# Down stages in slots, split halves made earlier, and another order of the first block-product step in a streaming encoder layer

## The chip, the core and the metric

The kernel runs on one core of one Trainium2 chip. Its time is the device time of one execution in microseconds (us), the median of several runs. TensorE (PE) multiplies, VectorE (DVE) and ScalarE (ACT) work elementwise and read the accumulators in PSUM, GpSimd (POOL) works elementwise on SBUF alone, and the queue of SyncE (SP) issues the DMAs. The engines run side by side, each in its own program order, and wait for each other by semaphores.

## The reference

One step of an encoder layer for 1056 rows (1024 of a prompt, 32 of a running stream), width 1024. Two SwiGLU feed-forward blocks (FFN) of inner width 2816 enclose a token mixer:

```python
def swiglu(h, w_gate, w_up, w_down):
    return (jax.nn.silu(h @ w_gate) * (h @ w_up)) @ w_down

def layer(x, lw, sb_fn, s0, gla_chunk):
    ...
    x = x + 0.5 * swiglu(rmsnorm(x, g_ffn1), w1g, w1u, w1d)
    mix, k, v, s = token_mixer(rmsnorm(x, g_mix), w_in, w_gate_up, ...)
    x = x + mix
    x = x + 0.5 * swiglu(rmsnorm(x, g_ffn2), w2g, w2u, w2d)
    return rmsnorm(x, g_final), k, v, s
```

The mixer (stick-breaking attention beside gated linear attention) is not touched by the change.

## The kernel before, in words

All data lie transposed: `x[d]` and `h[d]` (d of 8) hold 128 features by 1056 rows. A float32 value is kept as two halves, a rounded high one and the rest: ScalarE copies the high half, VectorE subtracts to get the low half, and a product is made of three matmuls (high by high, high by low, low by high). Such a pair of instructions is called a split (`split_to`, L96, its ScalarE copy at L100, its VectorE subtraction at L104; in slots L50 and L51).

An FFN has these stages.

*Opening.* The first pair of hidden tiles (f = 0 and 1) is multiplied plainly, row quarter by row quarter (`Opening`, matmuls at L292). Beside it the normed `x` is split into `h` and `X` (tiles `h` and `part`), and the sums T1, T3, T2, T4 of its blocks are made and split (`Halves.part`, sums L243, splits L104).

*Gate and up.* The other 20 hidden tiles are made in 20 steps (a gate step and an up step for each pair i = 1 to 10), each a seven-product block scheme (`Step`, matmuls L384): product p multiplies a weight sum with a block sum (`PRODUCTS`) and adds into one of four PSUM banks a, b, c, d. Products 1 and 2 share bank a, 7 and 4 share c, 5 and 3 share d, and 6 has b. `ORDER` is 1, 6, 7, 5, 2, 4, 3. After each product VectorE or ScalarE reads a bank (`after`): c1 after 1, u2 = c1 + b after 6 (L400), u3 = u2 + c after 7 (L403), outputs after 5, 2, 4 and 3. The second product of a bank adds to what stands there, so it must wait until the first has been read out. Within these steps the program order is written out by hand (`manual_schedule`): `Slots` is a list of work by product number, where `later(k)` puts work k products on. `slots.split` puts the ScalarE half at k and the VectorE half at k + 1. The weights' sums of the next step are made on GpSimd in the same way. In the first FFN the slots also carry the splitting of the mixer's weights (`Splits`: load, split, store to `win_split` and `wo_split`). Pairs 1 to 8 are kept as block sums in DRAM (`keep`, `part_spill`); the six plain tiles 0, 1 and 18 to 21 (`PLAIN`) go to `hid_spill` unsplit.

*Down.* Pairs 1 to 8, in four groups of two, are multiplied by the down weights in 16 steps (`DownStep`, matmuls L590, banks `pd_a` to `pd_d`), again of seven products, here of 12 matmuls. VectorE reads each bank (L579) and GpSimd adds (L608). Between the products stand the loads of later weights (`wraw`) and parts, the sums on GpSimd (L553 to L556) and the splits of the next step (`prep`). In the last group `plain_tile` and `plain_slab` load and split the six plain tiles (12 halves) and six slabs of their weights. This stage has no hand-written order: a scheduler places the instructions of each engine.

*Plain.* The six plain tiles are multiplied by their slabs (`pd`, L109 to L111). The second FFN ends with the closing norm.

Of the kernel before, what the change touches and what calls it, by code (L numbers as in the profile page):

```python
# [533 lines left out]
PLAIN = (0, 1, 18, 19, 20, 21)  # L534


class DownStep:
# [6 lines left out]
    def sums(self, raw):  # L544
# [6 lines left out]
        s1, s2, s3, s4 = s12[:, :w], s12[:, w:], s34[:, :w], s34[:, w:]  # L551
        self.src = raw, s12, s34
# [5 lines left out]
    def halves(self):  # L558
        S = self.S
        w = 2 * P  # L560
        raw, s12, s34 = self.src
        tag = ("S1", "A22") if self.odd else ("S2", "S3")
        wa = S.sr.tile([P, 2, 512], F32R, name=tag[0], tag=tag[0])
        wb = S.sr.tile([P, 2, 512], F32R, name=tag[1], tag=tag[1])
        ws = S.wp.tile([P, 2, 1024], F32R, name="whl", tag="w")
# [5 lines left out]
        self.W = {"A11": cut(wa, 0), "A12": cut(wa, 1), "A22": cut(wb, 0)}  # L571
        self.W.update({f"S{i + 1}": cut(ws, i) for i in range(4)})
# [39 lines left out]
class Down:  # L612
# [25 lines left out]
    def load_w(self, pool, name):  # L638
        t = pool.tile([P, 1024], F32, name=name, tag=name)
        self.S.nc.sync.dma_start(t, self.src[self.slab])  # L640
        self.slab += 1
        return t
# [1259 lines left out]
```

## Time and profile before

| what | value |
|---|---|
| time, median of 3 runs | 2134.49 us (2132.89 to 2135.83) |
| the profiled execution | 2135.43 us, span 2133.5 us |
| TensorE busy | 2058.4 us, 96% of the span |
| VectorE, ScalarE, GpSimd busy | 67%, 42%, 31% |
| mean granted clock of TensorE | 0.99 |
| first FFN: first `L384` matmul, first `L590`, first plain `pd` | 76.39, 496.86, 671.48 us |
| second FFN: the same | 1468.25, 1877.96, 2050.41 us |

The trace is of one execution. A row of the timeline has start, length, engine, line, operation, output and inputs, shapes and count; in brackets stands how long the engine was idle before it and what ended that. Matmul lengths overlap, so a product's time is the distance between starts.

### The profile page before, as it was taken

To read this page: it belongs to the slowest core of one execution; us is meant where nothing else is said; L and a number is where in the kernel's file an instruction comes from. 1 tells how busy PE (TensorE), PEld (TensorE's weight loads), DVE (VectorE), ACT (ScalarE), POOL (GpSimd) and SP (SyncE) were. 2 spreads that over 40 slices of the span, in tenths; PEclk is the share of its full clock that TensorE was granted. 3 is DMA by queue.
4 is the path that set the end of the run, shared out by engine and by line. 5 is a ranking of instruction groups with operands and counts; after the bars stand their busy time and mean duration, and the time that the engine had idled before them with its cause. 6 is when DMAs were issued, how large, how long until landed. Compare 5 with 4: busy or idle time off the path is not lost.

```text
span 2133.5 us, 38802 instructions
## 1 busy us (share of the span) xinstructions
PE 2058.4 (96%) x15636; PEld 1991.8 (93%) x15636; DVE 1438.7 (67%) x2205; ACT 886.8 (42%) x1618; POOL 655.3 (31%) x578
## 2 busy tenths in 40 slices
PE   7899999999999999999999999899999999999997
PEld 6899999999999988888989988899999999999997
DVE  6767777765786656286766688596666666467855
ACT  6544444442233443235555565353333433322333
POOL 0034433435773200111121201101343343357720
PEclk9999999999999999999999999999999999999999
DMA  5156776779653211113314152331243434597322
GB/s 175 55 212 249 254 259 250 248 257 386 246 194 115 76 67 60 44 64 86 91 49 134 54 182 75 106 109 49 108 155 138 152 132 151 188 376 290 113 65 82
DMA packets 128339, 325.03 MB, mean 152 GB/s; under 512 B 12097, under 2 KB 32865, under 8 KB 124833
## 3 DMA queue, kind: packets, MB, share of 16 engines
q1 hardware_dynamic: 128160, 322.56, 42.8%
q8 instruction: 123, 2.02, 0.4%
q14 instruction: 56, 0.45, 0.1%
HBM read 201.72 MB, written 114.03 MB: 148 GB/s over the span
## 4 chain that ended last, share of the span: by engine, by line
PE 80%; DVE 9%; issue 3%; DMA 3%; ACT 3%; POOL 2%; DVEq 0%; SPq 0%; ACTq 0%; POOLq 0%
PE acc_a L384 11%; PE acc_c L384 11%; PE acc_d L384 11%; PE acc_b L384 6%; PE acc L292 4%; PE pj L109 4%; PE pj L111 3%; PE pj L110 3%; PE pd_a L590 2%; PE pd_d L590 2%; PE pd_c L590 2%; PE pd L109 2%; PE pd L111 2%; PE pd L110 2%; DMA wraw<-hid_spill 2%
## 5 line engine op out<-in xcount | busy, mean ns | idle before, releaser
L384 PE MATMUL acc_a<-h,whl 128*128 128x264 f32 x1920 | 249.9, 286 | 8.4 <-DVE whl L104 8.4
L384 PEld LDWEIGHTS acc_a<-h,whl 128*128 128x128 f32 x1920 | 241.5, 190 | 8.6 <-DVE whl L104 8.6
L384 PE MATMUL acc_d<-part,S 128*128 128x264 f32 x1920 | 246.1, 284 | 0.0
L384 PEld LDWEIGHTS acc_d<-part,S 128*128 128x128 f32 x1920 | 238.4, 188 | 0.0
L109 PE MATMUL pj<-h,whl 128*128 128x352 f32 x576 | 204.7, 355 | 0.0
L111 PE MATMUL pj<-h,whl 128*128 128x352 f32 x576 | 189.9, 330 | 0.0
L110 PE MATMUL pj<-h,whl 128*128 128x352 f32 x576 | 188.3, 327 | 0.0
L434 POOL TENSOR_TENSOR x<-tc,x 128x528 f32<-128x528 f32 x60 | 100.7, 1678 | 181.4 <-DVE tc L433 139.9
L50 ACT ACTIVATE x<-x 128x528 fp32r<-128x528 f32 (+1 forms) x164 | 102.5, 635 | 113.8 <-issue 30.2
L51 DVE TENSOR_TENSOR x<-x 128x528 fp32r<-128x528 f32 (+1 forms) x164 | 129.9, 805 | 17.4 <-ACT x L50 17.4
L355 POOL TENSOR_TENSOR s<-wraw 128x512 f32<-128x512 f32 x38 | 58.1, 1529 | 225.9 <-DVE S L104 186.4
L384 PE MATMUL acc_c<-h,A 128*128 128x264 f32 x960 | 124.2, 285 | 0.0
L384 PE MATMUL acc_b<-h,S 128*128 128x264 f32 x960 | 124.2, 285 | 0.0
L384 PE MATMUL acc_c<-part,S 128*128 128x264 f32 x960 | 123.0, 284 | 0.0
L384 PEld LDWEIGHTS acc_c<-h,A 128*128 128x128 f32 x960 | 120.4, 188 | 0.0
L384 PEld LDWEIGHTS acc_b<-h,S 128*128 128x128 f32 x960 | 120.4, 188 | 0.0
L384 PEld LDWEIGHTS acc_c<-part,S 128*128 128x128 f32 x960 | 119.2, 188 | 0.0
L608 POOL TENSOR_TENSOR x<-x,u 128x528 f32<-128x528 f32 x64 | 98.7, 1549 | 53.0 <-DVE x L579 52.0
L109 PEld LDWEIGHTS pj<-h,whl 128*128 128x128 f32 x576 | 109.8, 191 | 4.8 <-issue 1.5
L50 ACT ACTIVATE S<-s 128x512 fp32r<-128x512 f32 x152 | 93.4, 623 | 46.9 <-PE acc_b L384 18.4
L51 DVE TENSOR_TENSOR S<-s,S 128x512 fp32r<-128x512 f32 x152 | 112.1, 738 | 0.0
L111 PEld LDWEIGHTS pj<-h,whl 128*128 128x128 f32 x576 | 109.2, 190 | 1.9 <-issue 1.0
(349 smaller groups left out, 4886.2 us busy)
## 6 DMA issues: line engine op xcount, KB each, us to landing
part_spill<-x SPq DMA_DIRECT2D x112, 528.0 KB, 3.4
h<-part_spill SPq DMA_DIRECT2D x64, 528.0 KB, 10.4
part<-part_spill SPq DMA_DIRECT2D x48, 528.0 KB, 10.6
win_split<-x SPq DMA_DIRECT2D x44, 512.0 KB, 3.4
whl<-win_split SPq DMA_DIRECT2D x22, 1024.0 KB, 4.9
wraw<-w1g SPq DMA_DIRECT2D x22, 512.0 KB, 5.3
wraw<-w1u SPq DMA_DIRECT2D x22, 512.0 KB, 6.3
x<-win SPq DMA_DIRECT2D x44, 256.0 KB, 3.1
```

What stands on the lines that cost most here:

```text
L50: self.later(k, lambda: nc.scalar.activation(hi, src, AF.Copy))
L51: self.later(k + 1, lambda: nc.vector.tensor_sub(lo, src, hi.bitcast(F32)))
L109: nc.tensor.matmul(out, w[:, 0, wsl], a[:, 0, asl], start=first, stop=False)
L110: nc.tensor.matmul(out, w[:, 0, wsl], a[:, 1, asl], start=False, stop=False)
L111: nc.tensor.matmul(out, w[:, 1, wsl], a[:, 0, asl], start=False, stop=last)
L292: nc.tensor.matmul(out, self.w[i](k, a), quarter(S, k, b, j), start=k == 0 and n == 0, stop=k == KT - 1 and n == 2)
L355: eng.tensor_add(self.s1, a21, a22)
L384: nc.tensor.matmul(t[:, s, :SW], w[:, a, ks], m(k, b, s), start=fresh and k == 0 and n == 0, stop=k == 3 and n == 2, skip_group_check=not ...
L434: nc.gpsimd.tensor_mul(two(hid), t, sg)
L590: nc.tensor.matmul(t[:, s, :SW], w[:, u, k * P : k * P + P], b[:, v, ss(s)], start=fresh and k == 0 and i == 0, stop=k == 1 and i == 2, sk ...
L608: nc.gpsimd.tensor_add(x[r][h], x[r][h], u)
```

## The change

- `FIRST`: the first gate step of each FFN makes its products in the order 1, 5, 2, 6, 7, 4, 3. The output of product 5's quarter is then read out after product 7.
- The sums T2 and T4, and the weights' sums of the first step, are emitted later or in another order. In the first FFN T2 comes behind the weights of product 5, T4 behind the Opening in both.
- In the down stages everything on TensorE, VectorE, ScalarE and SP, loads included, has a written order. The sums and splits of the next step come in two parts (`first`, `second`) by slots, between the products of the step before.
- Tiles 18 and 19 are split in gate and up, when they are made, and stored as halves (`hid_split`). In the second FFN tiles 0 and 1 and the six slabs are also split there, by `Splits`, as jobs of 512 or 528 columns (`halves_of`), and stored (`hid_split`, `w2d_split`); the down stage then loads the halves. The other splits of the last group stay, in slots.

The diff, cut:

```diff
+def halves_of(jobs):
+
+    out = []
+    for src, dst in jobs:
+        w = src.shape[-1] // 2
+        out += [(src[:, h * w : h * w + w], dst[:, :, h * w : h * w + w]) for h in range(2)]
+    return out
...
-        for n in range(2 * len(self.jobs)):
+        dma = self.S.nc.sync.dma_start
+        for n, (src, out) in enumerate(self.jobs):
             k = 5 * n // 2
-            buf = self.bufs[n % 2][:, :1024]
+            w = src.shape[-1]
+            buf = self.bufs[n % 2][:, : 2 * w]
             t = buf.rearrange("p (a n) -> p a n", a=2)
             hl = t.bitcast(F32R)
-            src, out = self.jobs[n // 2]
-            cols = slice(n % 2 * 512, n % 2 * 512 + 512)
-            dma = self.S.nc.sync.dma_start
-            slots.later(k, lambda buf=buf, src=src, cols=cols: dma(buf[:, 512:], src[:, cols]))
-            slots.split(hl[:, 0], hl[:, 1], buf[:, 512:], k + 2, lambda t=t, out=out, cols=cols: dma(out[:, :, cols], t))
+            raw = buf[:, w:]
+            slots.later(k, lambda raw=raw, src=src: dma(raw, src))
+            slots.split(hl[:, 0], hl[:, 1], raw, k + 2, lambda t=t, out=out: dma(out, t))
...
 ORDER = (1, 6, 7, 5, 2, 4, 3)
+FIRST = (1, 5, 2, 6, 7, 4, 3)
...
+            if "d" in A:
+                self.out(3, self.u3, A["d"])
...
+            if "c" in A:
+                self.out(3, self.u3, A["d"])
...
-            if f in PLAIN:
+            if f in PLAIN and f not in SPLIT:
...
+        if 2 * self.i in SPLIT:
+            q = {"B11": 0, "T1": 1, "B21": 2, "B22": 3}.get(name)
+            if q is not None:
+                out = self.S.hid2[PLAIN.index(2 * self.i + q // 2)][:, :, q % 2 * HALF : q % 2 * HALF + HALF]
+                self.keep(out, self.S.x[4 + q][:, :HALF])
+            return
...
-                for p in (6, 7, 5):
-                    prep(p)
+                prep(5)
+                between(4, 0)
+                prep(6)
+                prep(7)
...
     for k in range(4):
         H.part("T3", k, 1)
+    for k in range(4):
+        H.part("T4", k)
...
-            for n, p in enumerate(ORDER):
+            for n, p in enumerate(ORDER if t else FIRST):
...
+SPLIT = (18, 19)
...
-        nc.gpsimd.tensor_add(s1, a[3], a[2])
-        nc.gpsimd.tensor_sub(s2, s1, a[0])
-        nc.gpsimd.tensor_sub(s3, a[0], a[3])
-        nc.gpsimd.tensor_sub(s4, a[1], s2)
...
-        split_to(S, wa[:, 0], wa[:, 1], raw[:, :512])
-        split_to(S, ws[:, 0, :512], ws[:, 1, :512], s12)
-        split_to(S, wb[:, 0, :w], wb[:, 1, :w], raw[:, 2 * w : 3 * w])
-        split_to(S, ws[:, 0, 512:], ws[:, 1, 512:], s34)
...
+        nc.gpsimd.tensor_add(s12[:, :w], a[3], a[2])
+        nc.gpsimd.tensor_sub(s12[:, w:], s12[:, :w], a[0])
...
+        S.slots.split(self.wa[:, 0], self.wa[:, 1], raw[:, :512], k)
+        S.slots.split(self.ws[:, 0, :512], self.ws[:, 1, :512], s12, k + 1)
...
+        nc.gpsimd.tensor_sub(s34[:, :w], a[0], a[3])
+        nc.gpsimd.tensor_sub(s34[:, w:], a[1], s12[:, w:])
+        S.slots.split(self.wb[:, 0, :w], self.wb[:, 1, :w], a[2], k)
+        S.slots.split(self.ws[:, 0, 512:], self.ws[:, 1, 512:], s34, k + 1)
...
-            self.steps[0].sums(self.raw.pop(0))
+            self.steps[0].first(self.raw.pop(0), 1)
         elif p == 5:
             self.load_part(0, 6)
-        elif p == 2:
-            self.steps[0].halves()
...
-        for i, st in enumerate(self.steps):
-
-            def between(n):
-                if n == 0:
-                    self.load_step(i + 2)
-                if n == 1:
-                    self.prep(i + 1)
-                if st.g < last and n % 2 == 0 and 4 * (n // 2) + st.m < 7:
-                    self.load_part(st.g + 1, 4 * (n // 2) + st.m)
-                if st.g == last and n % 2 == 0 and n < 6:
-                    self.plain_tile(3 * st.m + n // 2)
-                if st.g == last and n == 5 and st.m > 1:
-                    self.plain_slab()
-
-            st.emit(between)
+        todo = [(lambda n=n: self.plain_tile(n)) for n in range(12)]
+        at = {}
+        for n, fn in enumerate(todo):
+            at[12 + n // 4, n % 4 * 2] = fn
+        for j, key in enumerate(((13, 1), (15, 0), (15, 1), (15, 2), (15, 3))):
+            at[key] = lambda j=j: self.plain_slab(j)
+        E = mybir.EngineType
+        with S.tc.manual_schedule(engines={E.PE, E.DVE, E.Activation, E.Pool, E.SP}):
+            for i, st in enumerate(self.steps):
+
+                def between(n):
+                    S.slots.run()
+                    if n == 0:
+                        self.load_step(i + 2)
+                    if i + 1 < len(self.steps):
+                        if n == 0:
+                            self.steps[i + 1].first(self.raw.pop(i + 1), 1)
+                        if n == 1:
+                            self.steps[i + 1].second(2)
+                    if st.g < last and n % 2 == 0 and 4 * (n // 2) + st.m < 7:
+                        self.load_part(st.g + 1, 4 * (n // 2) + st.m)
+                    if (i, n) in at:
+                        at[i, n]()
+                    S.slots.now += 1
+
+                st.emit(between)
+            self.plain_slab(5)
+            while S.slots.at:
+                S.slots.run()
+                S.slots.now += 1
...
-        raw = S.raw2.tile([P, 1024], F32, name="wraw2", tag="wraw2")[:, :HALF]
-        S.nc.sync.dma_start(raw, S.hidden[n // 2][:, cols])
-        t = self.tiles[n // 2]
-        split_to(S, t[:, 0, cols], t[:, 1, cols], raw)
-
-    def plain_slab(self):
+        t = self.tiles[n // 2][:, :, cols]
+        if PLAIN[n // 2] in SPLIT or PLAIN[n // 2] < 2 and self.done is not None:
+            S.nc.sync.dma_start(t.bitcast(F32), S.hid2[n // 2][:, :, cols])
+        else:
+            S.nc.sync.dma_start(t[:, 1].bitcast(F32), S.hidden[n // 2][:, cols])
+            S.slots.split(t[:, 0], t[:, 1], t[:, 1].bitcast(F32), 3)
...
-        split_to(S, w[:, 0], w[:, 1], r)
+        if self.done is not None:
+            S.nc.sync.dma_start(w.bitcast(F32), self.done[j])
+        else:
+            pool, name = (S.raw, "wraw") if j in (0, 1, 3, 5) else (S.raw2, "wraw2")
+            raw = pool.tile([P, 1024], F32, name=name, tag=name)
+            S.nc.sync.dma_start(raw, self.src[len(self.steps) + j])
+            S.slots.split(w[:, 0], w[:, 1], raw, 3)
...
-                    emit(parts(H))
+                    emit(parts(H, "T1", "T3"))
+                if j == 4:
+                    emit(parts(H, "T2"))
...
+            splits = Splits(S, halves_of(jobs), (S.x[2], S.x[3]))
...
-            down = Down(S, A["w2d"])
+            down = Down(S, A["w2d"], A["w2d2"])
+            jobs = [(S.hidden[i], S.hid2[i]) for i in range(2)] + [(A["w2d"][16 + j], A["w2d2"][j]) for j in range(6)]
+            splits = Splits(S, halves_of(jobs), (S.x[2], S.x[3]))
...
+                    emit(parts(H, "T1", "T3", "T2"))
+
+            gate_up(S, H, op, steps, lambda j, n: [], between, down.head, xs, splits.plan)
```

How instructions move. First VectorE in the first FFN, at the end of the Opening (`x<-x` are the block sums, `h` T2's and T4's splits, `whl` the weights of products 1 and 2, `S` and `A` weight sums, `hid` an output of the Opening). Before:

```order
L243 TENSOR_TENSOR x<-x 128x528 x6
L104 TENSOR_TENSOR h_84<-x,h_84 128x528
L104 TENSOR_TENSOR h_85<-x,h_85 128x528
L104 TENSOR_TENSOR h_86<-x,h_86 128x528
L243 TENSOR_TENSOR x<-x 128x528 x3
L104 TENSOR_TENSOR h_87<-x,h_87 128x528
L104 TENSOR_TENSOR h_88<-x,h_88 128x528
L104 TENSOR_TENSOR h_89<-x,h_89 128x528
L243 TENSOR_TENSOR x<-x 128x528 x2
L304 TENSOR_TENSOR hid<-sg,acc_615 128x528
L104 TENSOR_TENSOR h_90<-x,h_90 128x528
L104 TENSOR_TENSOR h_91<-x,h_91 128x528
```

and now, from the same place on:

```order
L253 TENSOR_TENSOR x<-x 128x528 x3
L314 TENSOR_TENSOR hid<-sg,acc_615 128x528
L113 TENSOR_TENSOR whl<-wraw,whl 128x1024
L113 TENSOR_TENSOR S_766<-s_764,S_766 128x512
L253 TENSOR_TENSOR x<-x 128x528 x3
L113 TENSOR_TENSOR h_84<-x,h_84 128x528
L113 TENSOR_TENSOR h_85<-x,h_85 128x528
L113 TENSOR_TENSOR h_86<-x,h_86 128x528
L253 TENSOR_TENSOR x<-x 128x528
L113 TENSOR_TENSOR S_788<-s_786,S_788 128x512
L314 TENSOR_TENSOR hid<-sg,acc_791 128x528
L113 TENSOR_TENSOR h_87<-x,h_87 128x528
```

Before, `whl` is the row behind these; now it stands third, and T4's sums and splits come further on.

TensorE in the first step, with product 7 (`acc_c` from `part`) and what follows it. Before, product 5 in `acc_d`:

```order
L384 MATMUL acc_c<-part_104,S_797 128x264 x6
L384 MATMUL acc_c<-part_105,S_797 128x264 x6
L384 MATMUL acc_d<-part_106,S_800 128x264 x6
L384 MATMUL acc_d<-part_107,S_800 128x264 x6
L384 MATMUL acc_d<-part_106,S_800 128x264 x6
```

and now product 4, in the bank of product 7:

```order
L394 MATMUL acc_c<-part_104,S_788 128x264 x6
L394 MATMUL acc_c<-part_105,S_788 128x264 x6
L394 MATMUL acc_c<-h_88,A_864 128x264 x3
L394 MATMUL acc_c<-h_89,A_864 128x264 x3
L394 MATMUL acc_c<-h_90,A_864 128x264 x3
```

VectorE there, now (`u_987` is u2, `u_1019` u3, `A` and `h` what product 4 needs, the rows at L51 the first piece of `win` and a weight sum of the next step):

```order
L113 TENSOR_TENSOR A_864<-wraw_529,A_864 128x512
L378 TENSOR_TENSOR s_867<-wraw,s_781 128x512
L113 TENSOR_TENSOR h_91<-x,h_91 128x528
L410 TENSOR_TENSOR u_987<-s_903,acc_b 128x528
L113 TENSOR_TENSOR S_869<-s_867,S_869 128x512
L51 TENSOR_TENSOR x<-x 128x512
L51 TENSOR_TENSOR S_933<-s_931,S_933 128x512
L413 TENSOR_TENSOR u_1019<-u_987,acc_c 128x528
L437 TENSOR_TENSOR x<-u_1019,acc_d 128x528
L437 TENSOR_TENSOR x<-u_987,acc_c 128x528
```

From the start of the list of now above, 33 short instructions and `whl` stand ahead of u3, the read-out of `acc_c`; before, u3 stood behind the splits of T2 and T3 and had two products to itself.

VectorE in the last group of the down stage of the first FFN (`whl` with `s`, `S` and `A` are splits of the next step's weights, `part_106` a slab, `h_85` a plain tile, the rows with `pd` read-outs). Before:

```order
L104 TENSOR_TENSOR whl<-s_7150,whl 128x512
L104 TENSOR_TENSOR whl<-s_7151,whl 128x512
L104 TENSOR_TENSOR part_106<-wraw,part_106 128x1024
L579 SCALAR_TENSOR_TENSOR u_7148<-pd_b,s_7127 128x528
L579 SCALAR_TENSOR_TENSOR tc<-pd_c,u_7148 128x528
L579 SCALAR_TENSOR_TENSOR x<-pd_d,x 128x528
L579 SCALAR_TENSOR_TENSOR x<-pd_a,x 128x528
L104 TENSOR_TENSOR S_7288<-wraw_7129,S_7288 128x512
```

and now:

```order
L600 SCALAR_TENSOR_TENSOR u_7291<-pd_b,s_7265 128x528
L51 TENSOR_TENSOR h_85<-h_85 128x528
L600 SCALAR_TENSOR_TENSOR tc<-pd_c,u_7291 128x528
L51 TENSOR_TENSOR S_7274<-wraw_7139,S_7274 128x512
L600 SCALAR_TENSOR_TENSOR x<-pd_d,x 128x528
L51 TENSOR_TENSOR h_85<-h_85 128x528
L51 TENSOR_TENSOR whl<-s_7270,whl 128x512
L600 SCALAR_TENSOR_TENSOR x<-pd_a,x 128x528
L51 TENSOR_TENSOR S_7275<-wraw_7139,S_7275 128x256
L600 SCALAR_TENSOR_TENSOR x<-pd_c,x 128x528
L51 TENSOR_TENSOR whl<-s_7271,whl 128x512
L51 TENSOR_TENSOR part_106<-wraw,part_106 128x1024
```

Three splits in a row ahead of two read-outs have become one or two splits behind each read-out.

## Rows read from the trace of the kernel before

**Rows 1.** Busy time by stretches: PE, PEld, DVE, ACT, POOL, clock, DMA.

```profile
85.20:496.80 411.60, 411.58 (x3358) 411.59 (x3359) 290.54 (x379) 174.79 (x290) 162.70 (x112) 0.99 0.69 247
496.80:671.50 174.70, 167.48 (x1347) 165.91 (x1346) 133.02 (x172) 52.51 (x90) 116.96 (x108) 0.99 0.64 233
...
1878.00:2050.40 172.40, 165.87 (x1346) 164.17 (x1344) 132.28 (x171) 52.37 (x90) 116.96 (x104) 1.00 0.64 232
...
1468.20:1878.00 409.80, 409.80 (x3363) 409.80 (x3362) 238.64 (x323) 147.64 (x239) 155.30 (x111) 1.00 0.40 148
```

**Rows 2.** Waits of TensorE: us in total, times, longest.

```profile
PE pd_c L590 <- DVE tc L579: 9.2, 8, 1.9
```

**Rows 3.** Timeline of TensorE, first step of the first FFN.

```profile
76.39 0.41 PE L384 MATMUL acc_a<-h,whl 128*128 128x264 f32 x2
85.22 5.00 PE L384 MATMUL acc_a<-h,whl 128*128 128x264 f32 x22 [8.42 <-DVE whl L104]
...
107.61 0.65 PE L384 MATMUL acc_a<-h,whl 128*128 128x264 f32 x4
```

**Rows 4.** Timeline of VectorE and GpSimd, same place.

```profile
71.26 3.80 DVE L243 TENSOR_TENSOR x<-x 128x528 f32<-128x528 f32 x6
...
83.94 1.22 DVE L104 TENSOR_TENSOR whl<-wraw,whl 128x1024 fp32r<-128x1024 f32 x1
...
86.50 1.27 POOL L355 TENSOR_TENSOR s<-wraw 128x512 f32<-128x512 f32 x1 [85.66 <-DVE S L104]
86.90 3.30 DVE L104 TENSOR_TENSOR part<-x,part 128x528 fp32r<-128x528 f32 x4
```

**Rows 5.** The chain that ended last, same product of two steps.

```profile
98.98 2.93 PE acc_a L384 x24
...
119.47 2.93 PE acc_a L384 x24
```

**Rows 6.** Stretches about waits; granted clock is the third number from the end.

```profile
85.20:89.80 4.60, 4.58 (x21) 4.59 (x22) 4.60 (x7) 0.00 (x0) 1.27 (x1) 0.50 0.17 59
540.40:543.80 3.40, 3.40 (x18) 3.40 (x17) 0.72 (x2) 0.00 (x0) 3.10 (x4) 0.50 1.03 403
634.00:645.00 11.00, 10.92 (x89) 10.92 (x90) 9.94 (x13) 3.05 (x6) 9.39 (x9) 1.00 0.28 91
1294.80:1301.50 6.70, 5.19 (x20) 5.12 (x21) 4.03 (x4) 0.71 (x2) 1.66 (x4) 0.50 0.06 9
```

**Rows 7.** Timeline of TensorE and VectorE, first step of the second FFN.

```profile
1468.25 3.09 PE L384 MATMUL acc_a<-h,whl 128*128 128x264 f32 x24
...
1480.13 0.70 DVE L424 TENSOR_TENSOR x<-u,acc_d 128x528 f32<-128x528 f32 x1 [2.21 <-PE acc_d L384]
...
1488.71 2.49 PE L384 MATMUL acc_a<-h,whl 128*128 128x264 f32 x19
```

**Rows 8.** Timeline of TensorE and VectorE, down stages, and a wait in the mixer.

```profile
496.86 1.62 PE L590 MATMUL pd_a<-h,S 128*128 128x264 f32 x12
...
539.24 2.10 PE L590 MATMUL pd_d<-part,whl 128*128 128x264 f32 x12 [2.07 <-DVE x L579]
...
630.84 1.75 DVE L104 TENSOR_TENSOR part<-wraw,part 128x1024 fp32r<-128x1024 f32 x1
...
634.08 1.75 PE L590 MATMUL pd_c<-h,S 128*128 128x264 f32 x12 [1.67 <-DVE tc L579]
...
671.48 0.43 PE L109 MATMUL pd<-h,part 128*128 128x352 f32 x1 [1.12 <-DVE x L579]
...
1296.31 1.11 PE L850 MATMUL tr<-consts,x 128*128 128x128 f32 x4 [3.17 <-POOL x L831]
...
1877.96 1.62 PE L590 MATMUL pd_a<-h,S 128*128 128x264 f32 x12
...
2050.41 0.43 PE L109 MATMUL pd<-h,part 128*128 128x352 f32 x1 [0.54 <-DVE x L579]
```

**Rows 9.** DMA issues of 496 to 672 us: KB each, median us to landing.

```profile
wraw<-w1d SPq DMA_DIRECT2D x19, 512.0 KB, 8.8
```

More of the change, by code (lines that the diff above doesn't have):

```diff
@@ L448, in form, with keep @@
             self.S.nc.vector.tensor_sub(src, x, y)
-        self.keep(name, src)
-    def keep(self, name, src):
+        self.keep(self.S.parts[self.i - 1, PARTS.index(name)], src)
+    def keep(self, out, src):
         S = self.S
-        out = S.parts[self.i - 1, PARTS.index(name)]
         S.n_kept = getattr(S, "n_kept", 0) + 1
@@ L542, in __init__, with first @@
         self.odd = m % 2
-    def sums(self, raw):
+    def first(self, raw, k):
         S, nc = self.S, self.S.nc
@@ L550, in sums, with second @@
         s34 = S.s32.tile([P, 512], F32, name="s34", tag="s2")
[L551 to L569 removed]
+        self.src = a, s12, s34
+        nc.gpsimd.tensor_add(s12[:, :w], a[3], a[2])
+        nc.gpsimd.tensor_sub(s12[:, w:], s12[:, :w], a[0])
+        tag = ("S1", "A22") if self.odd else ("S2", "S3")
+        self.wa, self.wb = (S.sr.tile([P, 2, 512], F32R, name=n, tag=n) for n in tag)
+        self.ws = S.wp.tile([P, 2, 1024], F32R, name="whl", tag="w")
+        S.slots.split(self.wa[:, 0], self.wa[:, 1], raw[:, :512], k)
+        S.slots.split(self.ws[:, 0, :512], self.ws[:, 1, :512], s12, k + 1)
+    def second(self, k):
+        S, nc = self.S, self.S.nc
+        w = 2 * P
+        a, s12, s34 = self.src
+        nc.gpsimd.tensor_sub(s34[:, :w], a[0], a[3])
+        nc.gpsimd.tensor_sub(s34[:, w:], a[1], s12[:, w:])
+        S.slots.split(self.wb[:, 0, :w], self.wb[:, 1, :w], a[2], k)
+        S.slots.split(self.ws[:, 0, 512:], self.ws[:, 1, 512:], s34, k + 1)
         cut = lambda t, i: t[:, :, i * w : i * w + w]
[L571 to L572 removed]
+        self.W = {"A11": cut(self.wa, 0), "A12": cut(self.wa, 1), "A22": cut(self.wb, 0)}
+        self.W.update({f"S{i + 1}": cut(self.ws, i) for i in range(4)})
     def emit(self, between):
@@ L612, with __init__ @@
 class Down:
-    def __init__(self, S, wd):
-        self.S, self.src = S, wd
-        self.slab = 0
+    def __init__(self, S, wd, done=None):
+        self.S, self.src, self.done = S, wd, done
         h, X = S.h, S.X
@@ L636, in load_part @@
             self.S.nc.sync.dma_start(self.part(g, n, k).bitcast(F32), self.S.parts[i - 1, n])
[L638 to L642, printed above, removed]
     def load_step(self, i):
         if i < len(self.steps):
-            self.raw[i] = self.load_w(*((self.S.raw, "wraw") if i % 4 < 2 else (self.S.raw2, "wraw2")))
-    def prep(self, i):
-        if i < len(self.steps):
-            self.steps[i].sums(self.raw.pop(i))
-            self.steps[i].halves()
+            pool, name = (self.S.raw, "wraw") if i % 4 < 2 else (self.S.raw2, "wraw2")
+            t = self.raw[i] = pool.tile([P, 1024], F32, name=name, tag=name)
+            self.S.nc.sync.dma_start(t, self.src[i])
     def head(self, p):
@@ L663, in head @@
             self.load_part(0, 5)
-            self.steps[0].sums(self.raw.pop(0))
+            self.steps[0].first(self.raw.pop(0), 1)
         elif p == 5:
             self.load_part(0, 6)
-        elif p == 2:
-            self.steps[0].halves()
+            self.steps[0].second(1)
     def strassen(self, xd):
@@ L710, in plain @@
         n = len(PLAIN)
-        while len(self.ws) < 6:
-            self.plain_slab()
         for c in range(NCH):
@@ L1505, in body @@
         S.wp = pool("wp", 2)
-        S.hidden, S.parts = A["hid"], A["parts"]
+        S.hidden, S.hid2, S.parts = A["hid"], A["hid2"], A["parts"]
         def ffn_pools(es, part, inner, between=None):
@@ L1533, in scales, with parts @@
             return [lambda d=d: H.scale(j, d) for d in range(KT)]
-        def parts(H):
-            return [lambda n=n, k=k: H.part(n, k, 0 if n == "T3" else 2) for n in ("T1", "T3", "T2", "T4") for k in range(4)]
+        def parts(H, *names):
+            return [lambda n=n, k=k: H.part(n, k, 0 if n == "T3" else 2) for n in names for k in range(4)]
         mix = lambda *ls: [fn for fns in zip(*ls) for fn in fns]
@@ L1786, in between @@
                 if j == 1 and n == 2:
-                    emit(parts(H))
-            gate_up(S, H, op, steps, lambda j, n: [], between, down.head, xs, lambda slots: None)
+                    emit(parts(H, "T1", "T3", "T2"))
+            gate_up(S, H, op, steps, lambda j, n: [], between, down.head, xs, splits.plan)
             down.strassen(xs)
```

9 lines of the change are left out of this document (4 added, 5 removed).

## The prediction

> **What bounds the kernel.** I read the table by stretches first [rows 1]: in both long gate-and-up stretches TensorE is busy to the last 0.02 us, in the two down stretches (496.8 to 671.5 and 1878.0 to 2050.4) it misses 7.2 and 6.5 us. So the change can give back only time in which TensorE stands still or runs at half clock. Next the waits of TensorE: `pd_c`, a bank of the down stages, waits eight times for VectorE's `tc`, 9.2 us in all [rows 2]. Then the timeline: between the Opening and the first block-product step of the first FFN TensorE makes two matmuls at 76.39 and the next at 85.22, 8.42 us later, when VectorE has made the low half `whl` [rows 3]. Both are program order on VectorE, not speed: at 71.26 it starts six subtractions for T3 and T2 and comes to `whl` only at 83.94 [rows 4]; at 630.84 it takes a slab's low half ahead of the `tc` for which TensorE waits until 634.08 [rows 8].
>
> **The terms, against the profiled run of 2135.43 us (span 2133.5), which is 0.9 above the median of 2134.49.**
>
> *Unit.* Seven products of 24 matmuls take 119.47 - 98.98 = 20.49 us [rows 5]: 2.93 a product, 0.12196 a matmul.
>
> *First FFN, first step.* Before, from its first matmul (76.39) to the next step's (107.61) it takes 31.22 us [rows 3], 10.73 over 20.49. The wait is 8.42 of that. The other 2.3 is the clock: 22 matmuls took 5.00 us [rows 3], and from 85.2 to 89.8 the granted clock was 0.50, the 1.2 GHz level [rows 6].
> Now `whl` comes sooner. VectorE's rows are the same up to the row at 71.26; from there the order has three subtractions, one `hid`, then `whl`: 4 x 0.63 (3.80 / 6) + 1.22 = 3.7 us [rows 4], so `whl` is done at 75.0, ahead of 76.39, and S1, the next in the list, at 75.6, ahead of product 5 at 79.3. The old wait goes.
> The new order of products brings a wait of its own. Product 4 adds into the bank `acc_c` that product 7 has just filled, and VectorE must first read it out as u3. Before, products 5 and 2 stood between them and gave 5.9 us for it; now nothing does. Product 7 ends at 76.39 + 5 x 2.93 = 91.0. From 71.26 to u3 VectorE has 33 short instructions and `whl`: 33 x 0.63 + 1.22 = 22.0, so it reaches u3 at 93.3 if it never stands. Three sums of the next step on GpSimd run beside that list; one of 1.27 us beside four splits made them 3.30 instead of 2.52 [rows 4], 0.8 more, so up to 2.4 for three, u3 at 95.7. With u3's own 0.70 [rows 7] product 4 waits for 3.0 to 5.4 us. I take 4.2, the middle. The bounds are 0.9 (VectorE ahead: 0.2 from a product's end at 1468.25 + 4 x 2.93 = 1479.97 to a read-out at 1480.13, and its 0.70, [rows 7]) and 8.4, the wait of before. T4's splits stand in the same list ahead of u3, so product 4 needs nothing later than u3.
> The clock was 0.50 for 3.4 us behind a wait of 2.07 and for 6.7 us about one of 3.17, and stayed at 1.00 behind one of 1.67 [rows 6, 8]. A busy engine loses half of such a time: 0 to 3.4; I take 2.0. Last, product 1 of the next step needs that step's `whl`, which stands on VectorE behind product 4's read-out and two splits and is done about when product 3 ends: 0.3, bounds 0 and 1.
> So 10.7 is replaced by 4.2 + 2.0 + 0.3 = 6.5: gain 4.2.
>
> *Second FFN, first step.* There was no wait: 1468.25 to 1488.71 is 20.46 [rows 7]. VectorE is busy 238.6 of 409.8 us in this stretch, against 290.5 of 411.6 in the first FFN [rows 1], so product 4 waits for the bare read-out, 0.9, and `whl` costs 0.3: loss 1.2, bounds 0.5 and 3.
>
> *Down stages.* From the first `pd_a` to the first plain `pd` it is 671.48 - 496.86 = 174.6 us in the first FFN and 2050.41 - 1877.96 = 172.45 in the second [rows 8]; 16 steps x 7 x 12 matmuls at 0.12196 are 163.9. So 10.7 and 8.5 are lost to waits, to the half clock at 540.4 (half of 3.4) and to slow restarts. In the new order each read-out stands on VectorE straight behind its product, with one split of the next step after most of them. A step lasts 10.24 us; VectorE has six read-outs of 0.70 and splits of 3 x 0.61 + 0.31 (1.22 for 1024 columns, [rows 4]), 6.3. The strictest need is u3 before product 4, two products (2.9 us) after product 7 has ended; behind one split VectorE is late by 1.3 at most. GpSimd is busy 117 of 174.7 us [rows 1], 7.3 a step; its sums for the next step come before its additions to `x` in each step, in time for ScalarE's fourth split. I leave 0.6 and 0.3 us (first plain `pd` behind slab splits): gains 10.1 and 8.2. Bounds: 0 left, and all of it.
> The weights of a step come on SP's queue with the parts of the next group. A piece of `w1d` lands 8.8 us after its issue (median of 19, [rows 9]); the fixed order issues it at least a step, 10.24, ahead, and a late one only delays ScalarE's first split, which has 8 us until the step that needs it.
>
> *Halves made in gate and up.* Four splits of 528 columns more in the first FFN (pair 18/19) and 20 of 512 or 528 in the second (4 for 18/19, 4 for 0/1, 12 for the slabs), each about 0.63 to 0.83 on VectorE [rows 4] and a split's first half on ScalarE, with a load and a store on SP. That is up to 17 us on VectorE beside products: the first FFN's stretch carries 52 such jobs with TensorE at 411.58 of 411.60 [rows 1]. Cost 0; without that cover up to 17. What they free in the down stages is in the terms above.
>
> Sum: -4.2 + 1.2 - 10.1 - 8.2 = -21.3. 2135.4 - 21.3 = 2114.1, less 0.9 for the median: **2113 us**.
>
> **A rule weighed.** VectorE's splits beside GpSimd took 0.83 instead of 0.63 [rows 4]; at that rate a down step's work on VectorE is 6.3 + 0.7 = 7.0 of 10.24 and the sum above holds. The Trainium skill, "GPSIMD Engine Reference", Key points, says that GpSimd shares its SBUF interfaces with VectorE and contends with instructions that have two SBUF inputs, as all splits have. It gives no size. Taken as full exclusion it speaks against an order in which both have work in every slot, and gives the second rival.
>
> **Rivals.**
> 1. *The first step gains all it can* (2108): u3 costs 0.9, the clock stays, `whl` 0.3; 9.5 instead of 4.2. For it: a wait of 1.67 did not cost the clock. Against: the count of 33, which standing still can only lengthen.
> 2. *VectorE bounds the last down group* (2120): in step 13 it has, beside 4.2 of read-outs, splits of weights (2.1), two tile halves (1.26) and a slab (1.22), in step 15 two tile halves and three slabs. If every split doubles, step 13 is 4.2 + 2 x 4.6 = 13.4, 3.2 over 10.24, of which a slack of 1.6 hides half. Two such steps in the first FFN, with the clock's 1.7, and a lesser one in the second keep 6 to 7 us. Against: before, four tile halves more lay in the first FFN's last group, in a worse order, and a wait of 1.67 there is the common size.
> 3. *The wait only moves* (2118): ScalarE and VectorE take the split of the first `win` piece ahead of the first step's last splits; if it lands late, u3 waits with it, the wait is 8.4 again and the clock low as before: gain 0, and 0.7 for the late split.
> 4. *Slower* (2140): a queue in fixed order cannot be overtaken, so ScalarE and VectorE stand when a piece of weights is late. The place is the first split of each down step. It decides once a piece lands some 17 us after its issue (10.24 ahead and 8 of slack, less 1.3 for both halves of the split); 0.85 us in each of 32 steps is 27. Against: the landing of 8.8, and DMA engines busy 64% in these stretches [rows 1].
>
> **How the numbers follow.** Forecast 2113: 0.56; rival 1: 0.13; rival 2: 0.14; rival 3: 0.12; rival 4: 0.05. The range, 2106 to 2122, holds the forecast and the first three with their errors and leaves out the fourth and the joint bad end of 2 and 3. A measurement of this kernel tells a change from none at about 0.2%, 4.3 us, so faster is below 2130.2: 0.93; same 0.03 (the joint bad end, where also the second FFN's bound of 3 falls due), slower 0.04.
>
> **What would show it.** No wait of `acc_a` for `whl` near 76; instead one of `acc_c` for `u` near 91, some 4 us in the first FFN and about 1 in the second, low clock after the first alone. Down stretches of 164 to 165 us with hardly a wait for `tc`. Gate and up without idle TensorE, in the second FFN too. Wrong would be: TensorE waiting for splits or DMAs inside the down steps, idle time in gate and up, or a `whl` that still comes late at 76.

## The result, and the profile after

The changed kernel takes 2117.57 us (median of 5 runs, 2115.83 to 2120.76), beside 2132.89 for the kernel before: a ratio of 0.9933, 95% interval 0.9913 to 0.9953, or 14.3 us less (10 to 19). The forecast was 2113, with a range of 2106 to 2122. The profiled execution took 2118.24 us, its span 2116.5.

The stages, each from the start of its first matmul to the start of the next stage's:

| stage, us | before | after | change | predicted |
|---|---|---|---|---|
| up to the first block-product step | 76.39 | 76.51 | +0.1 | 0 |
| gate and up, first FFN | 420.47 | 417.01 | -3.5 | -4.2 |
| down, first FFN | 174.62 | 168.15 | -6.5 | -10.1 |
| from there to the second FFN's first step | 796.77 | 791.41 | -5.4 | 0 |
| gate and up, second FFN | 409.71 | 411.03 | +1.3 | +1.2 |
| down, second FFN | 172.45 | 169.20 | -3.2 | -8.2 |
| the end | 83.1 | 83.2 | +0.1 | 0 |
| span | 2133.5 | 2116.5 | -17.0 | -21.3 |

The down stages gave 9.7 us of the 18.3 predicted. 5.4 us came from a part that the change does not touch; run e4 below shows that this part differs by as much between two executions of the kernel before. So the change itself is worth some 11.6 us of this pair of profiles.

The busy time by stretches of the changed kernel, in the columns of [rows 1]; the first and third row lie inside gate and up, the others are the down stages:

```profile
105.00:493.50 388.50, 388.50 (x3188) 388.50 (x3187) 280.17 (x360) 168.84 (x280) 157.57 (x107) 1.00 0.70 250
493.50:661.70 168.20, 165.46 (x1347) 164.28 (x1346) 117.27 (x168) 50.02 (x89) 119.48 (x110) 1.00 0.71 263
1488.00:1864.10 376.10, 376.10 (x3086) 376.10 (x3085) 240.90 (x317) 143.29 (x234) 147.93 (x103) 1.00 0.48 177
1864.10:2033.30 169.20, 165.63 (x1346) 164.22 (x1344) 109.68 (x163) 43.23 (x80) 118.77 (x108) 1.00 0.74 279
```

Gate and up has no idle TensorE behind its first step, in the second FFN too, though the new halves are made there. In the down stages VectorE has 117 and 110 us of work instead of 133 and 132, the clock is full (before, [rows 6] had 0.50 at 540.4), and TensorE stands for 2.7 and 3.6 us instead of 7.2 and 6.5. But it stands for something else than in [rows 2]. These are all its waits from 70 to 670 us (total, times, longest):

```profile
PE acc_c L394 <- DVE u L413: 5.0, 1, 5.0
PE pd_d L611 <- DMA part<-part_spill: 1.3, 2, 0.7
PE pd_a L611 <- DMA part<-part_spill: 0.7, 1, 0.7
PE pd_c L611 <- DMA part<-part_spill: 0.6, 1, 0.6
```

The eight waits for `tc` are gone. In their place the first down step waits four times for DMAs that bring `part`, 2.65 us in all, and again 2.65 in the second FFN, where TensorE also waits 0.80 us for VectorE's last read-out ahead of the plain products. Now the first step, in TensorE's timeline, which answers [rows 3] and [rows 7]; the last row is the second FFN's:

```profile
76.51 3.09 PE L394 MATMUL acc_a<-h,whl 128*128 128x264 f32 x24
...
88.24 3.07 PE L394 MATMUL acc_c<-part,S 128*128 128x264 f32 x24
96.29 5.00 PE L394 MATMUL acc_c<-h,A 128*128 128x264 f32 x24 [4.98 <-DVE u L413]
101.13 3.09 PE L394 MATMUL acc_d<-part,S 128*128 128x264 f32 x24
104.06 3.33 PE L394 MATMUL acc_a<-h,whl 128*128 128x264 f32 x24
107.22 2.97 PE L394 MATMUL acc_b<-h,S 128*128 128x264 f32 x23
...
1468.68 3.19 PE L394 MATMUL acc_c<-h,A 128*128 128x264 f32 x24 [0.80 <-DVE u L413]
```

The wait of 8.42 us for `whl` is gone. Product 4 waits 4.98 us for u3, and takes 4.84 instead of 2.93, because the clock is low behind the wait:

```profile
93.60:100.40 6.80, 4.11 (x19) 4.14 (x20) 3.25 (x4) 2.63 (x4) 1.38 (x1) 0.50 0.45 170
```

TensorE is busy for 4.11 us of this stretch, at 1.2 GHz, so it loses 2.06 us. VectorE's and GpSimd's timeline of the same place, answering [rows 4], says why u3 comes when it does:

```profile
73.86 1.22 DVE L113 TENSOR_TENSOR whl<-wraw,whl 128x1024 fp32r<-128x1024 f32 x1
...
77.52 2.98 DVE L113 TENSOR_TENSOR h<-x,h 128x528 fp32r<-128x528 f32 x3
...
91.51 0.69 DVE L410 TENSOR_TENSOR u<-s,acc_b 128x528 f32<-128x528 f32 x1
92.12 1.14 DVE L113 TENSOR_TENSOR S<-s,S 128x512 fp32r<-128x512 f32 x1
93.18 0.68 DVE L51 TENSOR_TENSOR x<-x 128x512 fp32r<-128x512 f32 x1
93.78 1.75 DVE L51 TENSOR_TENSOR S<-s,S 128x512 fp32r<-128x512 f32 x1
95.45 0.69 DVE L413 TENSOR_TENSOR u<-u,acc_c 128x528 f32<-128x528 f32 x1
...
91.10 1.61 POOL L368 TENSOR_TENSOR s<-s,wraw 128x512 f32<-128x512 f32 x1 [12.41 <-issue]
93.34 1.64 POOL L371 TENSOR_TENSOR s<-wraw,wraw 128x512 f32<-128x512 f32 x1 [0.63 <-DVE S L113]
```

No row of VectorE from 65 to 97 us has an idle time in brackets: it works through its list, and u3 is late because the list is long. The two splits of 1.14 and 1.75 us end at 93.26 and 95.53, each 0.55 us behind the end of a GpSimd sum (92.71, 94.98). The three splits at 77.52, beside the first sum, took 2.98 us; three of the same size with no sum beside them took 1.93 (at 87.21).

Last, SP's queue ahead of the first down step; `L546` loads x[0] to x[3], `L657` the parts:

```profile
468.13 0.51 SPq L103 DMA_DIRECT2D wo_split<-x  x1
471.67 0.51 SPq L475 DMA_DIRECT2D hid_split<-x  x1
475.35 1.77 SPq L546 DMA_DIRECT2D x<-x  x4
477.18 1.15 SPq L663 DMA_DIRECT2D wraw<-w1d  x2
478.37 8.95 SPq L657 DMA_DIRECT2D h<-part_spill  x8
488.17 4.80 SPq L657 DMA_DIRECT2D part<-part_spill  x4
```

The last store of pair 9's halves leaves at 471.67 from one of the two temporaries x[0] and x[1]. It has waited 3.0 us for VectorE's half. SP's next entry loads these two again and waits 3.1 us for that store. SP's waits from 465 to 480 us:

```profile
SPq L475 <- DVE x L51: 5.0, 2, 3.0
SPq L546 <- DMA hid_split<-x: 3.1, 1, 3.1
```

Behind these loads stand the weights and the parts. From 480 us on the DMA engines are full:

```profile
480.00:485.00 5.00, 5.00 (x44) 5.00 (x43) 1.24 (x3) 0.00 (x0) 0.00 (x0) 1.00 1.01 407
...
500.00:505.00 5.00, 3.50 (x23) 2.74 (x21) 2.00 (x5) 0.00 (x0) 1.70 (x1) 1.00 1.05 405
```

The share of 1.05 and some 400 GB/s hold until 505; the parts for which TensorE waits from 500 on come at the end of this train. The theory that the runs test: the train starts too late, and the stores of pair 9 make it so.

### The profile page after: what moved, and what is told of

Its sections match the earlier page's. It is cut to its first block, busy times and chain, and to the rows that moved or that the text cites. A ratio compares the mean times of both kernels' runs of the same rounds, so it can differ in the third digit from the quotient of the medians.

```text
span 2116.5 us, 38898 instructions
## 1 busy us (share of the span) xinstructions
PE 2054.9 (97%) x15636; PEld 1989.1 (94%) x15636; DVE 1424.6 (67%) x2211; ACT 883.0 (42%) x1624; POOL 659.3 (31%) x578
## 4 chain that ended last, share of the span: by engine, by line
PE 84%; DVE 7%; DMA 4%; issue 2%; ACT 2%; POOL 1%; SPq 0%; DVEq 0%; ACTq 0%; POOLq 0%
PE acc_c L394 11%; PE acc_a L394 10%; PE acc_d L394 10%; PE acc_b L394 5%; PE pd_d L611 4%; PE pd_a L611 4%; PE pd_c L611 4%; PE acc L302 4%; PE pj L118 4%; PE pj L120 3%; PE pj L119 3%; PE pd L118 2%; PE pd L120 2%; PE pd L119 2%; PE pd_b L611 2%
## 5 line engine op out<-in xcount | busy, mean ns | idle before, releaser
L50 ACT ACTIVATE x<-x 128x528 fp32r<-128x528 f32 (+1 forms) x188 | 117.0, 634 | 124.0 <-DVE x L467 32.5
L51 DVE TENSOR_TENSOR x<-x 128x528 fp32r<-128x528 f32 (+1 forms) x188 | 152.1, 823 | 18.5 <-ACT x L50 18.5
L51 DVE TENSOR_TENSOR S<-s,S 128x512 fp32r<-128x512 f32 x152 | 116.4, 766 | 0.0
L118 PEld LDWEIGHTS pj<-h,whl 128*128 128x128 f32 x576 | 110.0, 191 | 4.8 <-issue 1.5
L120 PEld LDWEIGHTS pj<-h,whl 128*128 128x128 f32 x576 | 109.1, 189 | 1.9 <-issue 1.0
L119 PEld LDWEIGHTS pj<-h,whl 128*128 128x128 f32 x576 | 110.1, 191 | 0.9
```

The source lines that it names most:

```text
L50: self.later(k, lambda: nc.scalar.activation(hi, src, AF.Copy))
L51: self.later(k + 1, lambda: nc.vector.tensor_sub(lo, src, hi.bitcast(F32)))
L118: nc.tensor.matmul(out, w[:, 0, wsl], a[:, 0, asl], start=first, stop=False)
L119: nc.tensor.matmul(out, w[:, 0, wsl], a[:, 1, asl], start=False, stop=False)
L120: nc.tensor.matmul(out, w[:, 1, wsl], a[:, 0, asl], start=False, stop=last)
```

## The experiments

Times are medians; a ratio is to the runs of before on the same chip, with its 95% interval. Stage lengths are read as in the table above. "Gate and up" and "down" stand for both FFNs, first and second.

**e1_loads_ahead**: x[0] and x[1] behind the parts.

```
                     if p == 1:
-                        for d in range(4):
+                        for d in (2, 3):
                             S.nc.sync.dma_start(S.x[d], xd[d])
                     tail(p)
+                    if p == 5:
+                        for d in (0, 1):
+                            S.nc.sync.dma_start(S.x[d], xd[d])
```

> Only the loads of x ahead of the down stages are moved: x[2] and x[3] are loaded first, x[0] and x[1] behind the parts. Theory A (in the changed kernel the last store of the halves of pair 9, which leaves from x[0] or x[1], holds back the loads of x, and behind them on SP's queue the weights and the parts): the loads behind it start some 3 us sooner, the four waits of the first down step for part DMAs (2.65 us in each FFN, with the slow restarts 4.4 to 4.5) go, each down stretch falls from 168.4 to 164 to 165 us, and the time falls by 7 to 9 us against the changed kernel, to 2109 to 2111. Theory B (the part loads are late because TensorE frees their places late, whatever stands ahead of them on the queue): the four waits stay within 0.5 us, the time stays within 1 us. Theory C (the sixteen DMA engines are full from there on, at 400 GB/s, and the order of the loads does not matter): the part waits shrink, and VectorE waits for x[0] and x[1] instead; less than 3 us gained.

2120.77 us, ratio 0.9938 (0.9922 to 0.9954); down 168.85 and 167.94. Theory C came: the part waits went, and in their place VectorE's first read-out that adds to x stood for x[1] (issued behind 493.4; the two loads landed 10.2 us after their issue, by the median), and TensorE behind it (VectorE's and TensorE's rows):

```profile
505.20 0.71 DVE L603 SCALAR_TENSOR_TENSOR x<-pd_d,x 128x528 f32<-128x528 f32 x1 [5.38 <-issue]
...
505.96 1.98 PE L614 MATMUL pd_d<-part,whl 128*128 128x264 f32 x12 [3.15 <-DVE x L603]
```

With the engines full, another order of the same bytes only chooses what is late. Theory A is neither shown nor refuted: the train did not get shorter ahead of its last needed load.

**e2_no_stored_pair**

```
-SPLIT = (18, 19)
+SPLIT = ()
```

> The halves of pair 9 (tiles 18 and 19) are no longer made and stored in gate and up; they are loaded raw and split in the last down group, as before the change. Theory A (the stores of these halves hold back the loads of x and of the parts): the waits for part DMAs in the first down step go in both FFNs, each of the down stretches loses 4 us there; the splits come back in the last group, four tile halves beside the read-outs, and cost 0 to 2 us in each. Time 2109 to 2114. Theory B (places freed late) and theory C (DMA engines full): the waits for part DMAs stay at 2.6 us in each FFN, time 2117 to 2121.

2113.77 us, ratio 0.9903 (0.9886 to 0.9920); down 165.39 and 164.85. No wait for a part is left. SP's queue:

```profile
467.75 3.12 SPq L546 DMA_DIRECT2D x<-x  x4
470.96 0.90 SPq L663 DMA_DIRECT2D wraw<-w1d  x2
474.73 6.17 SPq L657 DMA_DIRECT2D h<-part_spill  x8
```

The loads of x leave 7.6 us sooner, 7.3 counted to the first down matmul. Theory A holds. By the ratios this kernel and the changed one (e10) just touch, at 0.9920; the stages tell them apart. The four splits that came back to the last down group fill VectorE there (18.53 us of the 18.60 from 640.0 on), but cost TensorE only waits of 0.36 and 0.29.

**e9_two_loads_ahead**: a start between the two. The pair stays; x[2], x[3] and the weights go ahead of x[0] and x[1], all ahead of the parts.

```
                     if p == 1:
-                        for d in range(4):
+                        for d in (2, 3):
                             S.nc.sync.dma_start(S.x[d], xd[d])
                     tail(p)
+                    if p == 1:
+                        for d in (0, 1):
+                            S.nc.sync.dma_start(S.x[d], xd[d])
```

> The stored pair stays. On SP's queue x[2] and x[3], which no store of halves holds, and the weights of two down steps go ahead of x[0] and x[1]; the parts stay behind all of them. If what counts is when the DMA engines, full from then on at 400 GB/s, begin on the bytes that the first down step needs: these 3.2 MB of x and weights begin at 472.6 instead of 475.35, 2.7 us sooner, and the waits for parts (2.65 us in each FFN, 4.4 with the restarts) go nearly or wholly, as they did with 7.6 us of lead; down stretches 164 to 166 us. If the stored halves do harm in another way (their own bytes, the places of the parts): the part waits stay above 2 us.

2113.92 us, ratio 0.9916 (0.9903 to 0.9929); down 166.05 and 166.76. Two part waits are left in the first FFN, 1.35 us instead of 2.65, and one of 0.62 in the second, beside one of 0.75 for VectorE's x:

```profile
471.51 1.44 SPq L546 DMA_DIRECT2D x<-x  x2
473.04 0.94 SPq L666 DMA_DIRECT2D wraw<-w1d  x2
474.90 0.93 SPq L550 DMA_DIRECT2D x<-x  x2
```

Counted to the first down matmul of the first FFN, the train starts 16.84 us ahead in e3 (below), 18.17 in the changed kernel, 21.24 here and 25.44 in e2, as in the kernel before. TensorE's waits for DMAs there are 3.15, 2.65, 1.35 and 0 us. The first three carry the same stored halves, so it is the start of the train that the waits follow; "nearly or wholly" was too much for this lead.

**e3_product_between**

```
-FIRST = (1, 5, 2, 6, 7, 4, 3)
+FIRST = (1, 5, 6, 7, 2, 4, 3)
```

> The first block-product step in the order 1, 5, 6, 7, 2, 4, 3: product 2 stands between 7 and 4. Theory D (VectorE is a backlog there, it has no idle time from 65 to 97 us, and u3 comes when its list comes to it): in this order u3 stands two splits earlier in the list (0.7 and 1.75 us), so the wait of product 4 in the first FFN falls from 5.0 to about 2.7, and the half clock behind it stays or shortens; gain 2 to 4 us there. In the second FFN the wait of 0.8 goes. Theory E (the wait is what it is because nothing stands between products 7 and 4): with one product of 2.93 us between them the wait falls to 2.0 and the second FFN's to 0. Both: time 2112 to 2116; the place of u3 in VectorE's time (about 93.3 by D, unchanged 95.4 by E) tells them apart.

2114.12 us, ratio 0.9900 (0.9880 to 0.9920); gate and up 414.18 and 409.73. The wait is 2.71 us, and u3 starts at 93.09 instead of 95.45 (VectorE's row, then TensorE's):

```profile
93.09 0.69 DVE L413 TENSOR_TENSOR u<-u,acc_c 128x528 f32<-128x528 f32 x1
...
93.93 4.67 PE L394 MATMUL acc_c<-h,A 128*128 128x264 f32 x24 [2.71 <-DVE u L413]
```

Theory D: the wait shrank by the 2.3 us by which u3 moved up in VectorE's list. Product 2, of 2.93 us, took the place of product 7, so product 4 itself came no later. In the second FFN, with no backlog, the wait of 0.80 went, as both theories have it. Here the DMA waits of the first down step grew from 2.65 to 3.15, one of 0.46 for `h` among them: gate and up ended 2.9 us sooner.

**e6_t4_on_gpsimd**

```
-            nc.vector.tensor_sub(out, x, y)
+            (nc.gpsimd if name == "T4" else nc.vector).tensor_sub(out, x, y)
```

> Only the four subtractions for T4 ahead of the first step go from VectorE to GpSimd, in both FFNs; the order of products stays 1, 5, 2, 6, 7, 4, 3. Theory D (VectorE's backlog sets u3): four instructions of 0.63 us leave its list, 2.5 us; u3 starts at 92.9 instead of 95.45 and the wait of product 4 falls from 5.0 to 2.5, or to 3.5 if VectorE's splits slow down beside GpSimd. Theory E (nothing between products 7 and 4): the wait stays at 4 to 5 us. Time 2114 to 2117.

2120.88 us, ratio 0.9935 (0.9921 to 0.9950); gate and up 419.28 and 411.07, 2.3 us longer in the first FFN than in the changed kernel. Neither number came. u3 starts at 97.22, later than before the shift; product 4 waits 3.73 us, and product 2 now waits 2.62, for ScalarE. Four instructions fewer, and VectorE is slower (GpSimd's rows, then VectorE's, then ScalarE's):

```profile
78.69 5.28 POOL L253 TENSOR_TENSOR x<-x 128x528 f32<-128x528 f32 x3
84.61 1.71 POOL L253 TENSOR_TENSOR x<-x 128x528 f32<-128x528 f32 x1 [0.65 <-DVE x L253]
...
82.73 1.80 DVE L253 TENSOR_TENSOR x<-x 128x528 f32<-128x528 f32 x1
85.71 1.19 DVE L113 TENSOR_TENSOR h<-x,h 128x528 fp32r<-128x528 f32 x1
...
80.52 1.18 ACT L109 ACTIVATE h<-x 128x528 fp32r<-128x528 f32 x2 [2.46 <-POOL x L253]
...
84.55 0.59 ACT L407 ACTIVATE s<-acc_a 128x528 f32<-128x528 f32 x1
```

GpSimd ends at 83.97 and 86.32; VectorE's instruction, 0.70 us long elsewhere, ends at 84.53 and 86.90, 0.56 and 0.58 behind. VectorE's five instructions beside the four sums took 7.54 us in place of 4.36 in the changed kernel, 3.2 more; the four subtractions had taken it 2.5. A second cause is mixed in. A sum takes GpSimd 1.7 us instead of VectorE's 0.62, and ScalarE's copies of T4 wait for the sums (2.46, 0.57 and 1.08 us). Behind them in its list stands the read-out of bank a at 84.55, for which product 2 waits; in the changed kernel it came at 79.64. VectorE in turn stands 0.68 us for a copy of ScalarE's. So this run does not test VectorE's list alone.

**e7_both_mends** and **e8_three_mends**: `SPLIT = ()` with the order of e3; then also the line of e6.

> No stored pair (18, 19) and the first step in the order 1, 5, 6, 7, 2, 4, 3 together. If the two gains are separate, as theories A and D have it: gate and up of the first FFN at 414.2, of the second at 409.7, down stretches at 165.4 and 164.9; 2113.8 - 2.8 - 1.3 = 2109.7 us. If the earlier end of gate and up takes the lead away from the loads again: part waits of some 2 us return in the first down step, 2112 to 2114.

> As the run with both mends, and the subtractions for T4 on GpSimd. By theory D the wait of product 4 in the first FFN, 2.7 with product 2 between, falls to 0.2 to 1.2 and no half clock follows (it cost some 1.7): 3 to 4 us less than with both mends, 2106 to 2107. If GpSimd slows VectorE as much as it takes from it: no change, 2109.7.

e7: 2109.55 us, ratio 0.9885 (0.9868 to 0.9902); gate and up 415.34 and 409.73, down 165.33 and 164.85. The gains add up; only the half clock behind the wait of 2.71 lasted 6.8 us instead of the 3.4 of e3, which is the 1.2 us more in the first gate and up (e3's row, then e7's):

```profile
93.90:97.30 3.40, 3.37 (x15) 3.40 (x16) 3.06 (x5) 2.69 (x5) 0.62 (x1) 0.50 0.36 140
92.70:99.50 6.80, 5.98 (x27) 6.01 (x28) 4.82 (x8) 3.64 (x6) 1.27 (x1) 0.50 0.43 164
```

e8: 2107.72 us, ratio 0.9878 (0.9860 to 0.9896), not told apart from e7 by its interval: the wait for u3 went, but product 6 waited 2.9 us for the halves of T2. Most of it is ScalarE's half, which stood as in e6 behind T4's copies and their wait for GpSimd's sums:

```profile
PE acc_b L394 <- ACT h L109: 2.1, 1, 2.1
PE acc_b L394 <- DVE h L113: 0.8, 1, 0.8
```

Both are faster than before and than the changed kernel.

**e5_slots_alone**: no halves are made in gate and up.

```
-SPLIT = (18, 19)
+SPLIT = ()
-            down = Down(S, A["w2d"], A["w2d2"])
+            down = Down(S, A["w2d"])
-            gate_up(S, H, op, steps, lambda j, n: [], between, down.head, xs, splits.plan)
+            gate_up(S, H, op, steps, lambda j, n: [], between, down.head, xs, lambda slots: None)
```

> No halves are made in gate and up at all: pair 9 as in the run without a stored pair, and in the second FFN the tiles 0, 1, 18 and 19 and all slabs are loaded raw and split in the last down group, as before the change. What is left of the change is the fixed order of the down stages and the first step. Theory H (the fixed order alone gives the gain of the down stages; the first FFN's last group carries just this load of splits and its down stretch took 165.4 us): the second down stretch goes from 164.9 to 165.2 to 166, its gate and up stays at 411.0; time within 1.5 us of the run without a stored pair (2113.8). Theory I (making the halves ahead is what frees VectorE): the second down stretch goes back towards the 172.4 of before, by 4 us or more; time 2118 or more.

2117.50 us, ratio 0.9919 (0.9903 to 0.9936); gate and up 416.90 and 410.81, down 165.34 and 168.16. Between the two theories: against e2, the second down stage is 3.3 us longer and the end 1.5. VectorE has no room left in the last two steps (third number 19.94 of 20.00), the first plain product waits for its last read-out, and the clock is at 0.50 for 3.4 us from 2031.8 on:

```profile
2012.00:2032.00 20.00, 17.02 (x133) 16.39 (x132) 19.94 (x25) 8.29 (x13) 15.28 (x11) 1.00 0.21 71
```

```profile
2030.81 0.43 PE L118 MATMUL pd<-h,part 128*128 128x352 f32 x1 [2.67 <-DVE x L600]
```

Of the 7.6 us that e2 gains in this stage over before, the fixed order gives 4.3 and the halves made ahead 3.3. Making them costs 0.24 us in gate and up (410.81 to 411.05). The first FFN carries the same splits, and VectorE's last read-out is as late there (660.57, 2.1 us behind the last down product, as in the second); but the first plain product starts at 658.49, ahead of that read-out. What ties the two together in the second FFN alone is open.

**e4_before_again**

> The kernel before, profiled once more, for the part between the first down stage and the second gate and up, which the change does not touch. In the two profiles it took 796.8 us before and 791.4 after. Theory F (the 5.4 us are from one execution to the next, as the low clock and the wait for the wo halves fall at 1256 to 1377 us): this profile shows some other length, by 2 us or more off 796.8. Theory G (the change itself speeds that part up): 796 to 797.5 again, with the waits at 1266 to 1377 as before.

2128.71 us. From the first plain product to the second FFN's first step it is 789.30 us (TensorE's rows), against 796.77 in the first profile:

```profile
672.33 0.43 PE L109 MATMUL pd<-h,part 128*128 128x352 f32 x1 [1.14 <-DVE x L579]
...
1461.63 1.62 PE L384 MATMUL acc_a<-h,whl 128*128 128x264 f32 x12
```

Theory F came. Over all profiles of this study the part has 789 to 797 us, whatever the kernel. All the rest of the span is 1336.7 and 1337.5 us in the two profiles of before.

**e10_changed_again**

> The changed kernel itself once more, on the same chip and beside the same runs of before, for a comparison of medians and for the part between the first down stage and the second gate and up. Waits of 4.98 and 0.80 for u3 and of 2.65 twice for parts, as in its first profile; down stretches 168 to 169.2 us; the untouched part anywhere from 789 to 797 us.

2116.70 us, ratio 0.9933 (0.9920 to 0.9946); the waits again 4.97 and 0.80, four part waits of 2.65 us in the first FFN. In the second they are not 2.65 as expected: two of 1.48, beside one of 0.74 for VectorE's x. Down 167.93 and 168.26, the untouched part is 790.64, all the rest 1323.5 (1325.1 in the first profile). By all the rest the change gains 12 to 14 us, by the ratio 14.3.

## Why the prediction was right, and where not

*First FFN's first step.* Right in mechanism, 0.8 us short. The wait for u3 is 4.98 for 4.2, the clock costs 2.06 for 2.0, the next step's `whl` 0.23 (107.22 - 104.06 - 2.93) for 0.3: 7.3 in place of 6.5. u3 was counted to 93.3 to 95.7 and started at 95.45. The middle was too kind: GpSimd's three sums held VectorE's splits by 1.05, 0.45 and 1.07 us (2.98 for 1.93, 1.14 for 0.69, 1.75 for 0.68), 2.6 in all, where the middle had 1.2 and the upper end 2.4. By e3 it is VectorE's list that sets the wait, as the count had it, and not the missing product between 7 and 4, with which the prediction began.

*Second FFN's first step.* Loss 1.3 for 1.2.

*Down stages.* The waits for `tc` went as said. Without the stored pair (e2) 1.5 and 0.95 us are left over the 163.9, for 0.6 and 0.3: the term was 16.8 instead of 18.3, near enough. With it 4.3 and 5.3 are left.

*Halves made in gate and up, at cost 0.* This step failed. It held for VectorE, ScalarE and TensorE (0.24 us by e5). But only their time was weighed. The four stores of pair 9 are on SP's queue ahead of the loads for the first down step, and they leave from x[0] and x[1], which those loads fill again: 7.3 us of lead are lost (18.17 against 25.44), and e2 wins back 7.1 us in the two down stages (168.15 + 169.20 - 165.39 - 164.85; 5.95 against e10's profile). The prediction listed "TensorE waiting for splits or DMAs inside the down steps" among what would be wrong, and asked of the DMAs only whether a `w1d` piece lands in time. Of the lead, SP's waits give 3.0 us to the last store's wait for VectorE's half, ahead of the loads in the queue, and 3.1 to its landing.

*The rivals.* The first fell: u3 did not come cheap. The second is half true: in e2 VectorE is full in the last group of the first FFN and TensorE waits 0.65 us there; in e5 it costs 3.3 in the second. The third did not happen. The fourth had the right kind of mechanism, a queue that nothing overtakes, but the late load was another.

*The number.* The sum was off by 8.6 us in the down stages and 0.7 in the first step. 5.4 us from the untouched part, which owe nothing to the change, hid more than half of this: without them the profiled run would have come to 2123.6, outside the range, not 2118.2. That this profile lies inside is luck. By the ratio the change gains 14.3 us, two thirds of the 21.3 forecast.

*The rule weighed.* The rows show more than the 0.83 of [rows 4]: four VectorE instructions that met a GpSimd one ended 0.55 to 0.58 us after it. The Trainium skill, "SBUF — State Buffer", Summary: rules for kernel authors, says that where VectorE has two SBUF inputs while the GpSimd operation reads SBUF, the second to issue "fully blocks" until the first is done; these rows agree.

## What to carry to other kernels

A store that is added ahead of a stage is to be followed in three places: its engine time, its place in the issuing queue, and the buffer that it leaves from. Where, as here, the DMA engines are full up to the moment of need, the order of loads only chooses what is late; what helps is an earlier start. A sum that goes to another engine is to be followed to every list that waits for it, ScalarE's too. Before a stall is put down to the instruction order of one engine, look whether the engine that it waits for is ever idle: if not, shorten or reorder its list.

## What was not expected of the hardware

Work moved from VectorE to GpSimd made VectorE later: four subtractions less in its list, and u3 1.8 us later (e6), with ScalarE's share in it. A wait of 2.71 us left the clock at 0.50 for 3.4 us in one execution and 6.8 in another (e3, e7). The same 790 us of untouched program differ by 7.5 us between two executions of one kernel (e4).
